# A hybrid decoder trunk on one core: where the sums of the down weights are made, when the last loads are issued, and which engine copies the exponentials

## The chip, the core and the metric

The kernel runs on one core of a Trainium2 chip. A core has five engines that work side by side: TensorE (PE in the profile; its weight loads are PEld), VectorE (DVE), ScalarE (ACT), GpSimd (POOL) and SyncE (SP), which in this kernel issues every DMA from one queue, in order. Each engine takes its instructions in the order in which the program put them. The metric is the device time of one execution in microseconds.

## The reference

One layer of a decoder trunk for 1024 tokens of width 1024, in float32. Three token mixers run on one projection of the normalised input: an attention with a forget bias ("FoX", 8 heads of 64), a diagonal state space ("S5") and a gated linear recurrence ("HGRN2"). Their outputs are merged with sigmoid gates, then come an output projection, a cross attention over 256 memory rows, and a SwiGLU of inner width 2816.

```python
def swiglu(h, w_gu, w_d):
    a, b = jnp.split(h @ w_gu, 2, axis=-1)
    return (jax.nn.silu(a) * b) @ w_d

merged = (gates[:, :, 0] * (y_fox @ wb[:BRANCH_W])
          + gates[:, :, 1] * (y_s5 @ wb[BRANCH_W:2 * BRANCH_W])
          + gates[:, :, 2] * (y_hg @ wb[2 * BRANCH_W:]))
x = x + merged @ w_out[l]
x = x + cross_attention(rmsnorm(x, norm_x[l]), rmsnorm(mem, norm_mem[l]), ...)
x = x + swiglu(rmsnorm(x, norm_ffn[l]), w_gate_up[l], w_down[l])
```

## The kernel before

**Numbers.** Every large product is made from two parts of each factor: ScalarE copies a tile to its rounded high part (`act(hi, src, AF.Copy)`, line 264), and VectorE subtracts it from the tile, which leaves the low part (line 267, through line 253 and 244). Three 128x512 matmuls (high by high, high by low, low by high) make one step (line 388, and line 1983 in the feed-forward stages). All additions and subtractions stand on line 244 in the profile, all ScalarE operations on line 241, all matmuls on line 226, so the rows are told apart by tile names.

**Order.** The program is one long list that a compiler pass turns into a fixed order for each engine. Main work is written as generators, and filler generators (projections) are stepped between their pieces by `drive` and `pump`, by a running sum of planned matmul time (`self.pe`, in which a 512-column matmul counts 0.215 us). `later(us, fn)` puts a piece of work in when that sum has grown by so many us. All tiles in SBUF that are named `u` share 50 buffers of 4 KB per partition. A load waits until a buffer is free, and SP stands still meanwhile.

**Attention stage** (`fox_main`, line 737; 320 to 630 us). Per head and half of the tokens, for each of 4 or 8 key blocks j: TensorE makes scores `st`, ScalarE takes their exponential into `pf` (line 778), GpSimd copies it to the high part `pt` (line 781), VectorE subtracts to the low part (line 784), GpSimd adds the exponential to a running sum `facc`, and two blocks later TensorE multiplies `pt` with the values (`pv`). Before a unit, maxima of the scores go through a short VectorE chain (`mc`), are transposed (`mt`) and copied by ScalarE into a row operand (`q12`). After a pair of units, `facc` is split into `ah` and summed over partitions by small matmuls (`sm`, line 834), which `later(2.0, sums)` puts in (line 841).

**Gated merge** (`gates`, `gate`, `glu`, lines 1608 to 1672; some 950 to 1100 us). For three branches and eight output blocks, a stored gate is loaded, multiplied with a branch projection and added to the merge tile `mg`. GpSimd adds the second branch, VectorE the third. The output projection (`residual`) and the cross attention follow.

**Feed-forward, up** (`ffn_up`, line 2109). Two gate/up blocks are computed directly. The other 20 go through a seven-product scheme on quadrants (`PRODUCTS`, line 28): weights a11, s1, s2, s4, s3, a12, a22 with activations b11, t1, t2, b22, t3, b21, t4. `ffn_mix` makes t1 to t4 and their parts (tiles `t`, `th`, `tl`), `unit_prep` the weight sums of one block (tiles `sa`, `sb`) and their parts `wc`. While a block runs (`up_unit`), `after(n)` follows its product n: it prepares the next block's weights, or, behind the last block, loads and splits hidden rows (`h_load`, `h_split`, chunks by `H_AT`) and the first down weights (`dn_load`, `dn_prep`). The hidden rows and their mixes are stored to DRAM by `h_pair`, `h_pair2` and `h_store`.

**Feed-forward, down** (`ffn_down`, line 2232). The same seven products with four output blocks each, 28 weight blocks of 11 steps. For the sums s1, s2, s4 and s3, `dn_load` loads two sources and `dn_prep` adds or subtracts them on GpSimd (tiles `wr`) before the split into `wc`. The sums s1 and s2 are stored to DRAM, as s2 and s4 are made from them:

```python
DN_SRC = {"s1": ("a21", "a22"), "s2": ("s1", "a11"), "s4": ("a12", "s2"), "s3": ("a11", "a21")}
```

## Time and profile before

| what | value |
|---|---|
| time, median of 3 runs | 2147.52 us (2146.33 to 2148.11) |
| the profiled execution | 2145.49 us |
| its span on the core | 2143.7 us |
| TensorE busy | 2073.8 us, 97% of the span |
| VectorE, ScalarE, GpSimd busy | 1525.9, 814.1, 610.7 us |
| DMA traffic | 245.18 MB, mean 114 GB/s |

The busy time of TensorE is made from modelled ends of pipelined matmuls, so short gaps don't show in it; the number of matmuls that start in a stretch shows them. An idle time is put down to the instruction whose end released the engine. Where a wait row names an engine, that is the last of the things waited for.

### The profile page before, as it was taken

To read this page: it belongs to the slowest core of one execution; us is meant where nothing else is said; L and a number is where in the kernel's file an instruction comes from. 1 tells how busy PE (TensorE), PEld (TensorE's weight loads), DVE (VectorE), ACT (ScalarE), POOL (GpSimd) and SP (SyncE) were. 2 spreads that over 40 slices of the span, in tenths; PEclk is the share of its full clock that TensorE was granted. 3 is DMA by queue.
4 is the path that set the end of the run, shared out by engine and by line. 5 is a ranking of instruction groups with operands and counts; after the bars stand their busy time and mean duration, and the time that the engine had idled before them with its cause. 6 is when DMAs were issued, how large, how long until landed. Compare 5 with 4: busy or idle time off the path is not lost.

```text
span 2143.7 us, 26772 instructions
## 1 busy us (share of the span) xinstructions
PE 2073.8 (97%) x10044; PEld 1701.3 (79%) x10044; DVE 1525.9 (71%) x2221; ACT 814.1 (38%) x1268; POOL 610.7 (28%) x495
## 2 busy tenths in 40 slices
PE   8998999999999999999999999999999999989899
PEld 5887776776788888887888888878788888878677
DVE  8888898889845576536665576756878787866764
ACT  4113355556421222216334455534433333334231
POOL 4281204455531111000603000011432232425740
PEclk9999999999999999999999999999999999999999
DMA  4332120110210121124434533243222232269783
GB/s 162 137 103 75 51 86 21 40 50 30 79 54 30 50 69 55 59 98 171 159 102 144 197 90 108 79 165 125 92 97 102 99 123 98 99 228 356 267 292 132
DMA packets 102610, 245.18 MB, mean 114 GB/s; under 512 B 15816, under 2 KB 32200, under 8 KB 102480
## 3 DMA queue, kind: packets, MB, share of 16 engines
q1 hardware_dynamic: 102480, 243.46, 32.9%
q8 instruction: 79, 1.29, 0.2%
q14 instruction: 51, 0.42, 0.1%
HBM read 184.83 MB, written 57.41 MB: 113 GB/s over the span
## 4 chain that ended last, share of the span: by engine, by line
PE 65%; DVE 4%; issue 1%; DMA 1%; ACT 1%; POOL 1%; SPq 0%; DVEq 0%; POOLq 0%; ACTq 0%
PE pj L226 32%; PE fp L226 26%; PE hs L226 2%; PE xo L226 1%; DVE wc L244 1%; PE rs L226 1%; PE xs L226 1%; DVE hl L244 1%; PE ho L226 1%; POOL t L244 0%; PE hst L226 0%; PE pv L226 0%; PE st L226 0%; DVE tl L244 0%; DMA hr<-hb_d 0%
## 5 line engine op out<-in xcount | busy, mean ns | idle before, releaser
L226 PE MATMUL pj<-xh,wh 128*128 128x512 f32 x784 | 312.8, 404 | 6.7 <-ACT xh L241 5.3
L226 PE MATMUL pj<-xl,wh 128*128 128x512 f32 x784 | 314.1, 404 | 3.5 <-DVE xl L256 3.4
L226 PE MATMUL pj<-xh,wl 128*128 128x512 f32 x784 | 310.4, 399 | 0.0
L226 PE MATMUL fp<-hh,wc 128*128 128x512 f32 x644 | 196.5, 397 | 15.9 <-DVE wc L244 13.2
L226 PE MATMUL fp<-th,wc 128*128 128x512 f32 x640 | 208.2, 391 | 2.2 <-ACT th L241 2.2
L244 DVE TENSOR_TENSOR wl<-wr,wh 128x1024 fp32r<-128x1024 f32 (+2 forms) x138 | 166.1, 1204 | 52.1 <-ACT wh L241 50.2
L226 PEld LDWEIGHTS pj<-xh,wh 128*128 128x128 f32 x784 | 148.9, 190 | 39.6 <-ACT xh L241 5.8
L226 PEld LDWEIGHTS pj<-xl,wh 128*128 128x128 f32 x784 | 148.0, 189 | 35.4 <-DVE xl L256 5.8
L226 PE MATMUL fp<-fx,wc 128*128 128x512 f32 x720 | 173.0, 389 | 0.0
L226 PEld LDWEIGHTS pj<-xh,wl 128*128 128x128 f32 x784 | 148.4, 189 | 30.7 <-issue 2.2
L241 ACT ACTIVATE wh<-wr 128x1024 fp32r<-128x1024 f32 (+2 forms) x138 | 131.6, 957 | 76.6 <-DMA wr<-w_in 39.6
L226 PEld LDWEIGHTS fp<-hh,wc 128*128 128x128 f32 x644 | 123.1, 192 | 44.7 <-DVE wc L244 15.8
L226 PEld LDWEIGHTS fp<-fx,wc 128*128 128x128 f32 x720 | 135.2, 188 | 28.1
L244 DVE TENSOR_TENSOR wc<-wr,wc 128x512 fp32r<-128x512 f32 (+1 forms) x116 | 119.7, 1054 | 40.9 <-ACT wc L241 40.9
L226 PEld LDWEIGHTS fp<-th,wc 128*128 128x128 f32 x640 | 120.9, 189 | 27.8 <-ACT th L241 2.7
L244 POOL TENSOR_TENSOR acc<-acc,sq 128x512 f32<-128x512 f32 (+1 forms) x18 | 30.8, 1709 | 375.5 <-ACT sq L241 375.4
L226 PE MATMUL fp<-tl,wc 128*128 128x512 f32 x320 | 125.3, 392 | 1.6 <-DVE tl L244 1.6
L244 DVE TENSOR_TENSOR pt<-pf,pt 128x512 fp32r<-128x512 f32 (+1 forms) x96 | 94.1, 983 | 39.6 <-POOL pt L260 39.3
L244 POOL TENSOR_TENSOR fc<-fc,fs 128x512 f32<-128x512 f32 x40 | 57.3, 1433 | 220.3 <-ACT fs L241 220.3
L226 PE MATMUL fp<-hl,wc 128*128 128x512 f32 x280 | 111.1, 397 | 0.0
L260 POOL TENSOR_SCALAR pt<-pf 128x512 fp32r<-128x512 f32 (+1 forms) x96 | 68.8, 717 | 136.4 <-ACT pf L241 126.0
L241 ACT ACTIVATE wc<-wr 128x512 fp32r<-128x512 f32 (+1 forms) x116 | 76.9, 699 | 64.4 <-POOL wr L244 47.4
(429 smaller groups left out, 4841.2 us busy)
## 6 DMA issues: line engine op xcount, KB each, us to landing
wr<-w_in SPq DMA_DIRECT2D x48, 512.0 KB, 4.1
wr<-w_gu SPq DMA_DIRECT2D x44, 512.0 KB, 4.1
wr<-w_dn SPq DMA_DIRECT2D x36, 512.0 KB, 7.1
hr<-hb_d SPq DMA_DIRECT2D x35, 512.0 KB, 6.7
hb_d<-fc SPq DMA_DIRECT2D x44, 256.0 KB, 2.1
gz_d<-gz SPq DMA_DIRECT2D x20, 512.0 KB, 2.9
gate<-gz_d SPq DMA_DIRECT2D x20, 512.0 KB, 3.7
wr<-xo SPq DMA_DIRECT2D x17, 512.0 KB, 4.9
```

Of the source, the lines that this page charges most:

```text
L226: self.nc.tensor.matmul(out, lhsT, rhs, start=start, stop=stop)
L241: self.nc.scalar.activation(out=out, in_=in_, func=f, **kw)
L244: return (eng or self.nc.vector).tensor_tensor(out=out, in0=a, in1=b, op=op)
L260: (eng or self.nc.vector).tensor_scalar(out=out, in0=a, scalar1=s1, scalar2=s2, op0=op0, **kw)
```

## The change

1. **Sums of the down weights.** A new function `dn_mix(n)` takes one output block and two row pairs: one load of all four quadrants, four GpSimd operations that make s1, s3, s2 and s4 in place, and 4 us of planned time later one store to the DRAM tensor `ws_d`. 24 of them run in a chain, 9 us of planned matmul time apart, from the point behind the last `hg_main` on, while the first branch is being merged. `dn_load` then loads one source for every block, from `ws_d` or from the input, and `dn_prep` only splits. The stores of s1 and s2 and `dkeep` are gone.
2. **End of the up stage.** The loads of down block 0 and of the first two hidden chunks are issued before the last gate/up block, those of the other chunks one product earlier than before; the loads of blocks 1 and 2 come behind products 1 and 3; blocks 0 and 1 are split behind products 2 and 4. The b11 rows of a pair are stored at the end of the even block.
3. **Start of the up stage.** The four weight sums of the first scheme block are made on GpSimd, and the mixes 2 and 3 both follow the second block of the second half.
4. **Attention stage.** All high parts of exponentials are copied by ScalarE instead of GpSimd, and the row sums `sm` come 6 us instead of 2 us of planned time behind their unit.

```diff
-H_AT = {0: (0, 1), 1: (2,), 2: (3,), 3: (4,), 4: (5,)}
+H_AT = {-1: (0, 1), 0: (2,), 1: (3,), 2: (4,), 3: (5,)}
-DN_SRC = {"s1": ("a21", "a22"), "s2": ("s1", "a11"), "s4": ("a12", "s2"), "s3": ("a11", "a21")}
+MIXED = {"s2": 0, "s4": 1, "s3": 2, "s1": 3}
+SUM_AT = 6.0
+MIX_AT = (4.0, 9.0)
...
-                if j % 4 in self.hi_pool:
-                    self.ts(pt[:, 0, q0:512], pr, 1.0, 0.0, ALU.mult, ALU.add, self.nc.gpsimd)
-                else:
-                    self.act(pt[:, 0, q0:512], pr, AF.Copy)
+                self.act(pt[:, 0, q0:512], pr, AF.Copy)
...
-            self.later(2.0, sums)
+            self.later(SUM_AT, sums)
...
+        self.ws_d = self.dp.tile([4, 4, P, NPR, P], F32, name="ws_d")
+        self.later(MIX_AT[1], lambda: self.dn_mix(0))
         zt = []
...
-    def unit_prep(self, j):
+    def unit_prep(self, j, eng=None):
...
-        self.add(sa[:, 0], a21, a22)
+        self.add(sa[:, 0], a21, a22, eng)
...
                 else:
                     self.heven = c1
+                    self.h_store("b11", j // 2, c11)
...
-        prep = self.unit_prep(FF_CONV)
+        prep = self.unit_prep(FF_CONV, self.nc.gpsimd)
...
-                elif i < 3:
-                    self.ffn_mix(i + 1)
-                    next(prep)
+                elif i < 2:
+                    for m in ((1,), (2, 3))[i]:
+                        self.ffn_mix(m)
+                        next(prep)
...
+                if n in (1, 3):
+                    self.dn_load((n + 1) // 2)
                 for c in H_AT.get(n - 1, ()):
                     self.h_split("b11", c)
-                if n in (0, 2, 4):
-                    self.dn_load(n // 2)
-                if n == 4:
-                    self.dn_prep(0)
-
+                if n in (2, 4):
+                    self.dn_prep(n // 2 - 1)
+
+            if prep is None:
+                self.dn_load(0)
+                for c in H_AT[-1]:
+                    self.h_load("b11", c)
             yield from self.up_unit(j, after)
...
+    def dn_mix(self, n):
+
+        ob, k = n // 6, 2 * (n % 6)
+        m = min(2, NPR - k)
+        t = self.u("dm", F32, (P, 4, 2, P))
+        self.nc.sync.dma_start(out=t[:, :, 0:m], in_=self.io["w_dn"][ob][:, :, k:k + m].rearrange("q p k m -> p q k m"))
+        a11, a12, a21, a22 = (t[:, q, 0:m] for q in range(4))
+        G = self.nc.gpsimd
+        self.add(a22, a21, a22, G)
+        self.sub(a21, a11, a21, G)
+        self.sub(a11, a22, a11, G)
+        self.sub(a12, a12, a11, G)
+
+        def store():
+            self.nc.sync.dma_start(out=self.ws_d[ob][:, :, k:k + m].rearrange("q p k m -> p q k m"), in_=t[:, :, 0:m])
+        self.later(MIX_AT[0], store)
+        if n + 1 < 24:
+            self.later(MIX_AT[1], lambda: self.dn_mix(n + 1))
...
-        if a in DN_SRC:
-            op = ALU.add if a == "s1" else ALU.subtract
-            self.tt(big[0], big[0], big[1], op, self.nc.gpsimd)
-            self.tt(rem[:, 0], rem[:, 0], rem[:, 1], op, self.nc.gpsimd)
-            if a in self.ws_d:
-                self.dkeep.append((a, ob, big[0], rem))
```

## Rows read from the trace of the kernel before

**Rows 1.** The page's first part: busy us, share, instructions of each engine.
```profile
PE 2073.8 (97%) x10044; PEld 1701.3 (79%) x10044; DVE 1525.9 (71%) x2221; ACT 814.1 (38%) x1268; POOL 610.7 (28%) x495
```

**Rows 2.** Table of stretches: PE, PEld, DVE, ACT, POOL busy (started), clock, DMA share, GB/s.
```profile
500.00:550.00 50.00, 46.00 (x216) 36.09 (x216) 45.41 (x65) 25.09 (x43) 28.54 (x32) 1.00 0.09 32
950.00:1000.00 50.00, 49.73 (x226) 40.10 (x225) 26.50 (x39) 28.87 (x39) 0.00 (x0) 1.00 0.46 165
1000.00:1050.00 50.00, 50.00 (x222) 41.39 (x221) 35.79 (x39) 23.94 (x33) 32.89 (x14) 1.00 0.57 195
1500.00:1550.00 50.00, 46.19 (x196) 37.48 (x195) 44.47 (x53) 20.41 (x29) 22.65 (x13) 0.97 0.21 74
1600.00:1650.00 50.00, 50.00 (x222) 41.44 (x221) 40.08 (x53) 16.28 (x28) 19.14 (x13) 1.00 0.34 122
```

**Rows 3.** Tile fp, matmuls: min/median/max ns, first and last start us, shapes.
```profile
L226 PE MATMUL fp<-fx,wc x720: 387/389/397, 1519.8 to 1903.7; 128*128 128x512 f32 x180
L226 PE MATMUL fp<-hh,wc x644: 387/389/792, 1909.5 to 2139.4; 128*128 128x512 f32 x161
L226 PE MATMUL fp<-th,wc x640: 388/389/628, 1522.5 to 1906.4; 128*128 128x512 f32 x160
```

**Rows 4.** TensorE's waits, 1900 to 2144 us: total us, times, longest.
```profile
PE fp L226 <- DVE wc L244: 13.2, 6, 3.8
PE fp L226 <- ACT wc L241: 2.7, 1, 2.7
```

**Rows 5.** Table of stretches, columns as in rows 2: the hand-over.
```profile
1910.00:1920.00 10.00, 6.23 (x18) 4.76 (x18) 6.60 (x7) 1.99 (x3) 2.18 (x1) 0.66 0.97 324
```

**Rows 6.** Groups by form, 1906 to 2060 us: busy, mean ns, idle before, releasers.
```profile
L244 DVE TENSOR_TENSOR hl<-hr,hh 128x1024 fp32r<-128x1024 f32 x22 | 36.6, 1688 | 0.0
L244 DVE TENSOR_TENSOR wc<-wr,wc 128x1024 fp32r<-128x1024 f32 x19 | 35.6, 1872 | 25.4 <-ACT wc L241 25.4
...
L244 POOL TENSOR_TENSOR wr<-wr 128x1024 f32<-128x1024 f32 x15 | 39.8, 2656 | 57.3 <-DMA wr<-w_dn 52.9 <-DVE hl L244 4.4
```

**Rows 7.** Timeline at 1519 to 1531 us: start, length, instruction, idle before.
```profile
1526.97 0.50 PE L226 MATMUL fp<-th,wc 128*128 128x512 f32 x1 [2.25 <-ACT th L241]
...
1527.02 4.19 DVE L244 TENSOR_TENSOR tl<-t,th 128x1024 fp32r<-128x1024 f32 x2
...
1519.41 2.21 POOL L244 TENSOR_TENSOR t<-xr,t 128x512 f32<-128x512 f32 x1 [4.24 <-DVE t L244]
```

**Rows 8.** Groups by form in the attention stage, 320 to 630 us, three engines.
```profile
L244 DVE TENSOR_TENSOR pt<-pf,pt 128x512 fp32r<-128x512 f32 x48 | 62.0, 1294 | 31.1 <-POOL pt L260 30.9
...
L244 DVE TENSOR_TENSOR ah<-facc,ah 128x512 fp32r<-128x512 f32 x16 | 11.8, 740 | 0.2
...
L260 POOL TENSOR_SCALAR pt<-pf 128x512 fp32r<-128x512 f32 x48 | 36.5, 763 | 63.2 <-ACT pf L241 58.2 <-DVE ah L244 2.2 <-DVE pt L244 1.5
...
L244 POOL TENSOR_TENSOR facc<-facc,pf 128x256 f32<-128x256 f32 x16 | 11.8, 736 | 1.4 <-ACT pf L241 1.4
...
L241 ACT ACTIVATE ah<-facc 128x512 fp32r<-128x512 f32 x16 | 10.0, 625 | 0.7 <-DVE pt L244 0.5
```

**Rows 9.** TensorE's waits in the attention stage, 320 to 630 us.
```profile
PE sm L226 <- DVE ah L244: 8.1, 5, 2.3
PE mt L231 <- DVE mc L244: 7.9, 9, 1.7
...
PE pv L226 <- POOL pt L260: 0.5, 1, 0.5
```

**Rows 10.** The merge, 945 to 1200 us: a wait of SP's queue; a GpSimd group.
```profile
SPq L1601 <- DVE hoT L244: 25.8, 1, 25.8
...
L244 POOL TENSOR_TENSOR mg<-mg,gate 128x512 f32<-128x512 f32 x16 | 38.8, 2453 | 156.0 <-DVE gate L244 155.8 <-ACT yh L241 0.2
```

**Rows 11.** DMA issues: count, KB each, median us from issue to landing.
```profile
wr<-w_dn SPq DMA_DIRECT2D x36, 512.0 KB, 7.1
...
gate<-gz_d SPq DMA_DIRECT2D x20, 512.0 KB, 3.7
```

More of the change, by code (lines that the diff above doesn't have):

```diff
@@ L733, in fox_pre @@
         return out + [chain, rows]
-    hi_pool = (0, 1, 2, 3)
     def fox_main(self):
@@ L1430, in run @@
         self.hb_d = self.dp.tile([7, NPR, P, 512], F32, name="hb_d")
-        self.ws_d = {n: self.dp.tile([4, P, NPR, P], F32, name=f"{n}_d") for n in ("s1", "s2")}
         self.filler("xo", self.out_proj())
@@ L2023, in unit_prep @@
         sa = self.u("sa", F32, (P, 2, 4, P))
-        self.add(sa[:, 0], a21, a22)
+        self.add(sa[:, 0], a21, a22, eng)
         parts("s1", sa[:, 0])
         yield
-        self.sub(sa[:, 1], sa[:, 0], a11)
+        self.sub(sa[:, 1], sa[:, 0], a11, eng)
         parts("s2", sa[:, 1])
@@ L2030, in unit_prep @@
         sb = self.u("sb", F32, (P, 2, 4, P))
-        self.sub(sb[:, 0], a12, sa[:, 1])
+        self.sub(sb[:, 0], a12, sa[:, 1], eng)
         parts("s4", sb[:, 0])
         yield
-        self.sub(sb[:, 1], a11, a21)
+        self.sub(sb[:, 1], a11, a21, eng)
         parts("s3", sb[:, 1])
@@ L2093, in h_pair @@
         b11, b12, b22 = e[:, 0:512], e[:, 512:1024], o[:, 512:1024]
-        self.h_store("b11", i, b11)
         self.sub(ta[:, 0], b12, b11, G)
@@ L2150, in first @@
             ta, tb = self.u("ta", F32, (P, 2, 512)), self.u("tb")[:, 0:512]
+            self.h_store("b11", 0, e[:, 0:512])
             self.h_pair(0, e, o, ta)
@@ L2159, in ffn_up @@
         self.hraw, self.hx = {}, {b: [] for b in HX}
-        self.draw, self.dw, self.dkeep = {}, {}, deque()
+        self.draw, self.dw = {}, {}
         for j in range(FF_CONV, NFF):
@@ L2201, in dn_load @@
         a, ob = PRODUCTS[s // 4][0], s % 4
-        big, rem = [], self.u("wr", F32, (P, 2, 3, P))
-        for n, src in enumerate(DN_SRC.get(a, (a,))):
-            ap = self.ws_d[src][ob] if src in self.ws_d else self.io["w_dn"][ob][QUAD[src]]
-            big.append(self.u("wr", F32, (P, 8, P)))
-            self.nc.sync.dma_start(out=big[n], in_=ap[:, 0:8])
-            self.nc.sync.dma_start(out=rem[:, n], in_=ap[:, 8:NPR])
+        big, rem = self.u("wr", F32, (P, 8, P)), self.u("wr", F32, (P, 3, P))
+        ap = self.ws_d[ob][MIXED[a]] if a in MIXED else self.io["w_dn"][ob][QUAD[a]]
+        self.nc.sync.dma_start(out=big, in_=ap[:, 0:8])
+        self.nc.sync.dma_start(out=rem, in_=ap[:, 8:NPR])
         self.draw[s] = big, rem
     def dn_prep(self, s):
-        while self.dkeep:
-            a, ob, big, rem = self.dkeep.popleft()
-            self.nc.sync.dma_start(out=self.ws_d[a][ob][:, 0:8], in_=big)
-            self.nc.sync.dma_start(out=self.ws_d[a][ob][:, 8:NPR], in_=rem[:, 0])
-        if s >= 4 * len(PRODUCTS):
+        if s >= 4 * len(PRODUCTS) or s in self.dw:
             return
-        a, ob = PRODUCTS[s // 4][0], s % 4
         big, rem = self.draw.pop(s)
-        if a in DN_SRC:
-            op = ALU.add if a == "s1" else ALU.subtract
-            self.tt(big[0], big[0], big[1], op, self.nc.gpsimd)
-            self.tt(rem[:, 0], rem[:, 0], rem[:, 1], op, self.nc.gpsimd)
-            if a in self.ws_d:
-                self.dkeep.append((a, ob, big[0], rem))
         hi, lo = (self.u("wc", F32R, (P, 8, P)) for _ in range(2))
         r = self.u("wc", F32R, (P, 2, 3, P))
-        self.split(big[0], hi, lo)
-        self.split(rem[:, 0], r[:, 0], r[:, 1])
+        self.split(big, hi, lo)
+        self.split(rem, r[:, 0], r[:, 1])
         self.dw[s] = hi, lo, r
```

## The prediction

> **What bounds the kernel now.** I read the page first: TensorE is busy 2073.8 of 2143.7 us [rows 1], so only its idle time can be won, about 70 us. A busy share hides part of that, since a 128x512 matmul is recorded as 389 ns long [rows 3], so I counted starts. The table of stretches shows 222 starts in 50 us where nothing stops TensorE [rows 2], which is 0.2252 us each. Then I looked where the count falls or the engine idles: the attention stage (320 to 630 us), the first products of the gate/up blocks (1500 to 1550) and the down projection (1900 to the end). The gated merge (950 to 1100) runs at 50.00 of 50 from 1000 on: TensorE is its bound, and VectorE, ScalarE and GpSimd have room there [rows 2]. Last I read who ended TensorE's idle time in each place, and what that engine did.
>
> The two feed-forward stages can be counted exactly. The up products are 20 blocks of 84 matmuls, 1680, from 1519.8 to 1906.4 and the length of one pitch [rows 3]: 1680 x 0.2252 = 378.3 us of 386.8, so 8.5 us are lost. The down products are 28 blocks of 33, 924 matmuls, which follow until 2139.4 [rows 3]: 924 x 0.2252 = 208.1 of 233.0, so 24.9 us are lost. Of these the wait rows name 13.2 + 2.7 [rows 4]. The rest is smaller gaps, and the clock: between 1910 and 1920, after idling, the granted clock was 0.66 and 18 matmuls started [rows 5], where 44 is the full rate. A stop costs more than its own length here.
>
> **Down projection: sums made earlier, second loads and stores gone.** Today 16 of the 28 weight blocks (s1, s2, s4, s3) are added from two loads on GpSimd before they are split. These sums took 2.66 us for 128x1024, and waited mostly for weight loads; VectorE's low part, which waits for ScalarE's high part, which waits for the sum, took 1.87 us [rows 6]. These low parts are what TensorE waits for [rows 4]. The change removes 32 GpSimd instructions, 16 second loads and 8 stores of 704 KB, about 17 MB, from a stage whose DMA share was 0.97 in the stretch shown [rows 5]. What remains per block of 33 x 0.2252 = 7.43 us is one 704 KB load, a ScalarE split and two VectorE low parts, 1.87 us and, for the 128x384 remainder, no more than that. VectorE's other work is six subtractions for hidden rows per product of four blocks, 1.5 per block at 1.69 us or less [rows 6]. Together that is 6.3 us of 7.43 at today's stretched durations, so nothing is late next in steady state.
>
> **Down projection: its beginning.** Of the 24.9 us the hand-over at 1906 to 1918 is the largest piece. The load of weight block 0 and of the first two hidden chunks moves ahead of the last gate/up block, whose 84 x 0.2252 = 18.9 us then cover it. The loads of blocks 1 and 2 and of the other hidden chunks move one product (2.7 us) earlier. The split of block 0 moves from the fifth product to the third, and block 1 is split inside this stage as well. On SP's queue these loads pass the stores of the last pair, which now stand ahead of some of them. The stores of b11 move to the end of the even block, where SP can stand until product 7 is evacuated; what is queued behind is the next weight load, three products away, so it costs nothing. VectorE gets two more low parts in these 18.9 us, but no next block is prepared then. I keep 3.4 us lost of 24.9 and take **-21.5 us**. Bounds: -24.9 (no loss left), and -11 if only the steady part or only the beginning is cured.
>
> **First up products.** TensorE stops for 2.25 us on the mixed activations th, then on tl, and VectorE's last two subtractions of that mix end only at 1531.2, sharing time with GpSimd [rows 7]. The change takes four VectorE additions for the first block away and puts them on GpSimd, at up to 2.21 us each by its row of that form [rows 7]. It issues mixes 1, 2 and 3 after the first and second matmul block instead of the first, second and third, 24 x 0.2252 = 5.4 us earlier for the last. Needed are 4.2 us (1531.2 less 1527.0, when TensorE wanted the first of them), and GpSimd is busy 22.65 of 50 us there [rows 2]. I take **-5 us** of 8.5; bounds +2 (GpSimd's additions queue ahead of its part of the mixes) and -8.5.
>
> **Attention stage: ScalarE copies.** GpSimd's 96 copies (a 512 one took 0.763 us) go to ScalarE, where the same form of copy took 0.625 us [rows 8]. Half of them are 512 wide, 48 x 0.625 = 30 us; the others are 128 to 384 wide, between 0 and 30 us, say 20. ScalarE is busy 25.1 of 50 us [rows 2]; 50 us more over 310 us make it about 33. VectorE's subtraction behind it took 1.294 us, while the same form in another place took 0.740 [rows 8]; at most 48 x 0.55 = 27 us of VectorE time come free, and GpSimd's running sum of the same tiles stays, so I count on half. TensorE itself waited only 0.5 us for these copies [rows 9]: it gains through VectorE's order. It waited 7.9 us for mc, a short chain on VectorE [rows 9]; I take half, 4 us. On ScalarE the next exponential and the row copies q12 queue behind each new copy, 0.6 us. The row sums sm, which cost 8.1 us because VectorE had not yet written ah, with 2.3 us the longest [rows 9], are issued 4 us of matmul time later (SUM_AT 2 to 6); I take all 8 us. Together **-12 us**. Bounds: +2 if every unit's rows come later (16 units x 0.6 = 10 us given back, and nothing for mc), and -25 if VectorE's relief also closes gaps too short for the wait rows.
>
> **Gated merge: the cost.** 24 mixes are added, each one load and one store of 512 KB at most (11.5 MB each way) and four GpSimd instructions of 128x256: 0.736 us each by the nearest form [rows 8], 1.23 by half of the strided 512 add that took 2.45 us in this stage [rows 10]; 71 to 118 us in all, over some 250 us. Each takes one of 50 buffers for a while, and SP issues it between the gate and weight loads. TensorE is what hides it, and SP has stood still 25.8 us on one store here [rows 10], in a stretch in which TensorE was still busy 49.73 of 50 [rows 2]. I take **+2.5 us**; bounds 0 and +25.
>
> Where GpSimd works beside it, VectorE's subtraction of two SBUF tiles is stretched from 0.740 to 1.294 us [rows 8]. The Trainium skill (SBUF — State Buffer, section "Who interferes with whom") says that a VectorE instruction with two SBUF inputs and a GpSimd instruction that reads SBUF exclude each other. The trace agrees in direction; by that rule the new sums delay VectorE in the merge, which is rival (d).
>
> **Sum.** -21.5 - 5 - 12 + 2.5 = -36.0 us. The profiled execution took 2145.49 us (span 2143.7, the rest around it) and gives 2109.5; the median of the runs is 2.0 above it, so **2111.5 us**.
>
> **Rivals.** (a) ScalarE takes GpSimd's place in the attention stage: rows and exponentials are late behind the copies, and the stage comes out at its +2: 2125.5. For it: ScalarE is in order and its work rises by a third. Against: it has 17 of 50 us left. (b) VectorE is freed more than I count, -25 there: 2098.5. For it: 1.294 against 0.740. (c) The down stage is cured by half, since hidden rows or the first blocks are late instead of sums: +10.5, 2122. (d) VectorE becomes the merge's bound: it is busy 26.5 and 35.8 us per 50 [rows 2], some 156 of 250; if 118 us of GpSimd time shut it out in full, that is 274, 24 more than there is, 2133 to 2135. Against: the lower price gives 227, which fits. (e) Slower: SP's queue becomes the pace of the merge. SP waits in order, so between a mix's load and its store it may issue nothing: a landing of 3.7 us as for the gates or 7.1 as in the crowded down stage [rows 11], 2.9 to 4.9 us of sums, and up to one add of 2.45 ahead of them, 6.6 to 14.5 us. Mixes come every 9 us of planned matmul time, in which a 512 matmul counts 0.215: with 0.2252 and half a step of 1.4 us that is 10.1. At 13.5 us the queue falls behind by 3.4 x 24 = 82 us; less a lead of 25.8 us that is 56 us: 2165. It makes the kernel slower than before from 12.8 us per mix. Against it: loads are issued far ahead here, as the 25.8 us show.
>
> **Chances.** Forecast 0.52, (a) 0.15, (b) 0.13, (c) 0.07, (d) 0.06, (e) 0.07. Range: 2096 to 2131, which takes in (a), (b), (c) and most of the forecast's bounds, and leaves out (d) and (e), 0.13, with some of the tails. A measurement of this kernel tells about 0.2%, 4 us. Faster 0.91, same 0.03 (an (e) that just balances), slower 0.06.
>
> **What will show it.** The starts from the first to the last down product should span about 211 us, with a DMA share well below 0.97 and no granted clock near 0.66. The two stops on th and tl should shrink under 2 us together. In the attention stage sm should leave TensorE's waits, VectorE's 512 subtraction should fall to about 1.0 us, and ScalarE should be busy about 33 of 50. In the merge the busy time per 50 us should stay as it is. I am wrong if q12 or pf take over in the attention stage, if weight loads end TensorE's idle time in the merge, or if wc still ends it in the down stage.

## The result and the profile after

The changed kernel takes **2232.03 us** (median of 4 runs, 2230.73 to 2234.11) against 2147.82 before (4 runs): a ratio of 1.0384, interval 1.0363 to 1.0405. It is slower by 84 us where 36 us of gain were forecast. Its profiled execution took 2232.75 us, with a span of 2230.9.

The page of after, busy time and two of its 40 slices:

```profile
PE 2077.9 (93%) x10044; PEld 1705.4 (76%) x10044; DVE 1493.2 (67%) x2217; ACT 860.2 (39%) x1364; POOL 566.6 (25%) x467
...
PE   8998999899999999990299999999999999999999
...
PEclk9999999999999999995599999999999999999999
```

TensorE does the same 10044 matmuls in nearly the same busy time as in [rows 1], and its share falls from 97% to 93%: the new time is idle time, and the slices say where. Two of them, the 19th and 20th from the left, have almost no matmul in them, at half the granted clock. That is the gated merge. The table of stretches there (columns as in [rows 2]; the x of a stretch counts every instruction that lies in it, also those that began before it or end behind it), and who ended the waits of TensorE and of ScalarE:

```profile
990.00:1050.00 60.00, 15.77 (x66) 11.72 (x64) 11.35 (x14) 6.66 (x9) 31.43 (x47) 0.67 0.67 214
1050.00:1100.00 50.00, 0.00 (x0) 0.00 (x0) 0.00 (x0) 0.00 (x0) 30.41 (x46) 0.50 0.65 203
...
PE pj L228 <- ACT wh L243: 96.0, 1, 96.0
...
ACT wh L243 <- DMA wr<-w_glu: 88.7, 1, 88.7
```

In [rows 2] the same place has 222 matmuls in 50 us. Here one stop of 96.0 us stands: TensorE waits for ScalarE's high part of a weight block, and ScalarE waits 88.7 us for that block's load. For fifty microseconds only GpSimd works. The load isn't slow; it has not been issued. SP's queue in order of time (start, length, instruction), and its waits from 990 to 1110:

```profile
992.13 0.38 SPq L348 DMA_DIRECT2D wr<-w_glu  x1
...
993.39 2.82 SPq L2207 DMA_DIRECT2D dm<-w_dn  x3
1003.83 6.61 SPq L2216 DMA_DIRECT2D ws_d<-dm  x3
...
1097.84 1.85 SPq L2216 DMA_DIRECT2D ws_d<-dm  x2
1099.74 1.03 SPq L348 DMA_DIRECT2D wr<-w_glu  x2
...
SPq L2216 <- POOL dm L246: 59.8, 23, 3.7
...
SPq L2216 <- DMA dm<-w_dn: 18.5, 7, 3.9
```

Between one weight load at 992.13 and the next at 1099.74 SP issues nothing but the loads and stores of the mixes, and stands at the stores for 59.8 + 18.5 us. But for the load of the first one, at 964.53, all 24 mixes lie in one block of the queue, ahead of the weights that TensorE needs next.

The reason can be read in the code. The mixes are started with `later`, each of them puts the next one on the same list, and the next `finish()` that is called without a tag flushes that list:

```python
    def tick(self, flush=False):
        while True:
            due = [x for x in self.late if flush or x[0] <= self.pe]
            if not due:
                return
```

With `flush` the due time isn't looked at, and the loop goes on until the list is empty. The first `self.finish()` behind the start of the merge therefore runs mix 0, its store, mix 1, its store, and so on to mix 23 at a single point of the program. The description of the change, a chain in steps of 9 us of planned time, is what the constants say and not what the code does.

The rest of the profile, by stage. The table gives the start of a matmul in each trace less the start of the same matmul before, split into what each stage adds (us): the attention up to the last scores matmul, the stage behind it up to the last ho, the merge up to the last yh product, from there to the first matmul xs of the cross attention, the cross attention up to the first up product, the up products, the down products. "Ahead" is what had gathered at the first scores matmul. Up to there the kernels that differ only behind it run the same program, and yet lie between 0.0 and +2.9, so that 2 to 3 us of a single trace are not read as an effect; what returns in several kernels is.

| kernel | ahead | attention | to ho | merge | to xs | to up | up | down | sum |
|---|---|---|---|---|---|---|---|---|---|
| after | +1.7 | 0.0 | +5.2 | **+100.6** | +1.1 | 0.0 | +2.3 | **-23.5** | +87.3 |
| e1_spread | +1.4 | -1.0 | +5.2 | +22.7 | +22.0 | +1.6 | +1.1 | -23.5 | +29.5 |
| e7_late_store | +0.5 | -2.1 | +6.7 | +22.6 | +5.5 | +1.6 | +1.0 | -23.5 | +12.2 |
| e10_three_steps | +0.5 | -1.0 | +5.2 | +19.9 | +6.6 | 0.0 | +2.3 | -23.5 | +10.0 |
| e8_pool_store | +2.1 | -0.9 | +6.7 | +19.1 | +1.5 | 0.0 | +2.2 | -23.5 | +7.2 |
| e14_no_sums | +2.0 | -1.0 | +6.8 | **+2.0** | +3.9 | 0.0 | +1.1 | -23.5 | -8.8 |
| e11_best | +2.9 | -4.4 | +4.8 | +20.8 | +5.5 | +1.6 | +0.7 | -23.5 | +8.4 |
| e12_mix_in_cross | +1.7 | -4.5 | +4.9 | 0.0 | +0.1 | +5.7 | -0.3 | -23.5 | **-15.9** |
| e16_down_only | +2.8 | +1.6 | 0.0 | 0.0 | 0.0 | +8.4 | -0.2 | -23.5 | -10.9 |
| e2_act_only | +0.6 | -4.5 | +3.2 | 0.0 | +0.2 | +1.5 | 0.0 | +1.6 | +2.7 |
| e3_sum_only | +2.9 | +4.5 | +5.1 | 0.0 | 0.0 | 0.0 | -0.1 | +1.4 | +13.8 |
| e5_up_start | +0.4 | 0.0 | 0.0 | 0.0 | 0.0 | 0.0 | +1.1 | +1.4 | +2.8 |
| e15_mix_order | 0.0 | 0.0 | +0.1 | 0.0 | +0.5 | 0.0 | -0.7 | +0.2 | -0.1 |

**Down.** This part did what was meant. The tiles of the up and down products in after (as in [rows 3]), three stretches of the down stage, and under them the 50 us of the hand-over in the kernel before:

```profile
L228 PE MATMUL fp<-hh,wc x644: 388/389/389, 2017.4 to 2226.7; 128*128 128x512 f32 x161
...
L228 PE MATMUL fp<-th,wc x640: 388/389/628, 1631.0 to 2017.2; 128*128 128x512 f32 x160
...
2000.00:2050.00 50.00, 50.00 (x222) 41.44 (x221) 33.36 (x33) 24.26 (x33) 10.51 (x7) 1.00 0.80 287
2030.00:2040.00 10.00, 10.00 (x46) 8.29 (x45) 4.64 (x5) 3.86 (x5) 0.00 (x0) 1.00 1.02 378
2040.00:2050.00 10.00, 10.00 (x46) 8.29 (x45) 4.28 (x5) 5.86 (x9) 0.00 (x0) 1.00 1.04 391
```

```profile
1900.00:1950.00 50.00, 43.54 (x181) 35.19 (x181) 33.58 (x28) 19.79 (x28) 25.19 (x14) 0.93 0.91 332
```

The hand-over has no gap (2017.2, then 2017.4), the full count of 222 in 50 us stands from the first stretch, and the longest matmul of that group took 389 ns where [rows 3] had 792. From the last up product to the last down product there are 209.5 us instead of 233.0: 23.5 us won, in this and in every kernel of the table that has the part. That is all there was to win: 924 matmuls in 209.5 us are one per 0.2267 us, and the trace has three starts per 0.68 us where nothing stops TensorE. The DMA share was not what held the stage: over 50 us it is 0.80 where the kernel before has 0.91, but two stretches of 10 us reach 1.02 and 1.04 with no matmul lost. How much of the 23.5 us is the sums made earlier and how much the loads issued earlier was not run apart.

**Attention and up products.** Neither gained. TensorE's waits from 320 to 630 in after, VectorE's subtraction there, two stretches of it, the longest stop of the stage behind, and the first waits of the up products (1620 to 1660):

```profile
PE mt L233 <- DVE mc L246: 4.4, 6, 1.3
PE mx L228 <- DVE pmx L709: 3.3, 1, 3.3
PE pv L228 <- DVE pt L246: 2.7, 3, 2.1
...
PE sm L228 <- DVE ah L246: 1.6, 1, 1.6
...
L246 DVE TENSOR_TENSOR pt<-pf,pt 128x512 fp32r<-128x512 f32 x48 | 48.9, 1022 | 25.7 <-ACT pt L243 25.4
...
410.00:420.00 10.00, 7.92 (x29) 5.68 (x30) 7.59 (x18) 3.67 (x7) 1.36 (x3) 0.66 0.13 52
...
440.00:450.00 10.00, 6.75 (x27) 5.43 (x26) 9.30 (x14) 2.25 (x4) 3.35 (x3) 0.83 0.01 2
...
PE hst L228 <- ACT hbT L243: 3.0, 1, 3.0
...
PE fp L228 <- ACT th L243: 3.4, 1, 3.4
PE fp L228 <- DVE tl L246: 1.6, 1, 1.6
```

The signs that were named came: sm fell from 8.1 to 1.6 us and the 512 subtraction from 1.294 to 1.022 us [rows 8, 9]. The time didn't: mx and pv wait instead, two stretches ran at a granted clock of 0.66 and 0.83 where the kernel before has 1.00, and a stop of 3.0 us on hbT is new.

### The profile page after: what moved, and what is told of

It is laid out like the page before. It is cut to its first block, busy times and chain, and to the rows that moved or that the text cites. A ratio compares the mean times of both kernels' runs of the same rounds, so it can differ in the third digit from the quotient of the medians.

```text
span 2230.9 us, 26945 instructions
## 1 busy us (share of the span) xinstructions
PE 2077.9 (93%) x10044; PEld 1705.4 (76%) x10044; DVE 1493.2 (67%) x2217; ACT 860.2 (39%) x1364; POOL 566.6 (25%) x467
## 3 DMA queue, kind: packets, MB, share of 16 engines
q8 instruction: 79, 1.29, 0.2%
## 4 chain that ended last, share of the span: by engine, by line
PE 55%; POOL 3%; DVE 3%; DMA 2%; ACT 1%; issue 0%; SPq 0%; POOLq 0%; ACTq 0%; DVEq 0%
PE fp L228 26%; PE pj L228 24%; POOL dm L246 3%; DMA dm<-w_dn 2%; PE hs L228 1%; PE xo L228 1%; PE xs L228 1%; PE rs L228 1%; PE ho L228 0%; DVE tl L246 0%; DVE xr L258 0%; DMA wr<-xv 0%; DVE fx L246 0%; PE xt L233 0%; PE hst L228 0%
## 5 line engine op out<-in xcount | busy, mean ns | idle before, releaser
L243 ACT ACTIVATE wh<-wr 128x1024 fp32r<-128x1024 f32 (+2 forms) x138 | 131.7, 957 | 165.2 <-DMA wr<-w_glu 88.7
L228 PE MATMUL fp<-hh,wc 128*128 128x512 f32 x644 | 191.5, 389 | 0.0
L246 DVE TENSOR_TENSOR wc<-wr,wc 128x512 fp32r<-128x512 f32 (+1 forms) x116 | 107.1, 942 | 31.3 <-ACT wc L243 31.3
L246 POOL TENSOR_TENSOR dm<-dm 128x256 f32<-128x256 f32 (+1 forms) x96 | 64.8, 685 | 165.9 <-DVE wl L246 106.0
L228 PE MATMUL pj<-zh,wh 128*128 128x512 f32 x32 | 13.5, 425 | 96.0 <-ACT wh L243 96.0
L246 POOL TENSOR_TENSOR facc<-facc,pf 128x256 f32<-128x256 f32 (+1 forms) x64 | 71.1, 1110 | 119.8 <-ACT pf L243 114.0
```

What stands on the lines that cost most here:

```text
L228: self.nc.tensor.matmul(out, lhsT, rhs, start=start, stop=stop)
L243: self.nc.scalar.activation(out=out, in_=in_, func=f, **kw)
L246: return (eng or self.nc.vector).tensor_tensor(out=out, in0=a, in1=b, op=op)
```

## The experiments

Two questions were open. Is the slowdown the order (the flush, SP's queue), or the work (GpSimd's sums, the transfers)? And do the parts without the mixes give what was forecast? The theory after the comparison was: the flush makes nearly all of it, and without it the change is worth some 30 us. The rival: the work itself doesn't fit into the merge.

### The flush taken away

e1_spread: the mixes get a list of their own, which goes by the due time alone.

```diff
+    def spread(self, us, fn):
+        self.slow.append((self.pe + us, fn))
...
             due = [x for x in self.late if flush or x[0] <= self.pe]
+            due += [x for x in self.slow if x[0] <= self.pe]
...
-        self.later(MIX_AT[0], store)
+        self.spread(MIX_AT[0], store)
```

> The changed kernel, with the 24 mixes on a list of their own that is due by planned matmul time alone and that the end of the first branch does not flush; all else as in the change. Theory 1 (the flush put all mixes in one block ahead of the next weight loads on SP's queue): TensorE's 96 us wait in the merge goes, the time is 2232 less about 102, so 2128 to 2136. Theory 2 (the mixes themselves cost, through GpSimd time, shared SBUF access or DMA traffic in the merge): spread out they cost the same sum, and the time stays above 2180.

Measured: 2175.14 us (4 runs), ratio 1.0117, interval 1.0099 to 1.0136, between the two theories. So the flush alone is worth some 57 us of the 84, and the kernel is still slower than before. SP's waits of 990 to 1340 in e1_spread:

```profile
SPq L2222 <- POOL dm L246: 93.9, 22, 8.7
SPq L2222 <- DMA dm<-w_dn: 89.8, 21, 9.2
```

SP stands 183.7 us at 24 stores, 7.7 us each, with the weight and gate loads behind it. The stores came from 991.3 to 1263.8, one per 11.8 us, where the plan wanted one per 10.1. This is the wait of rival (e) of the prediction, SP at a store in front of loads; what it costs is shown by the kernels that take it away.

### SP kept from standing still

Three kernels take the waiting away from SP in three ways. e7_late_store issues the store 15 us of planned time behind the load; e10_three_steps moves the sums behind the load as well; e8_pool_store issues the store on GpSimd's own queue.

```diff
-MIX_AT = (4.0, 9.0)
+MIX_AT = (15.0, 9.0)          # e7_late_store
...
-        self.spread(MIX_AT[0], store)
+        self.spread(12.0, sums)   # e10_three_steps, with MIX_AT = (24.0, 9.0)
+        self.spread(MIX_AT[0], store)
...
-            self.nc.sync.dma_start(out=self.ws_d[ob][:, :, k:k + m]...
+            G.dma_start(out=self.ws_d[ob][:, :, k:k + m]...   # e8_pool_store
```

> The changed kernel with the mixes spread over the merge as in e1_spread, and each mix's store put on SP's queue 15 us of planned time behind its load instead of 4, so that the sums are done when SP comes to it. Nothing else differs: the same bytes, the same GpSimd work. Theory A (what is left of the slowdown in e1_spread, 2175.1 us, is SP standing in front of a store whose sums GpSimd has not made yet, with weight and gate loads queued behind it): SP's waits for GpSimd's dm, 93.9 us in the stretch 990 to 1340 of e1_spread, fall under 20 us, and the shift against the kernel before at the start of the first up product falls from +52 to about +10; 2130 to 2140 us. Theory B (the price is the work itself: 24 loads and stores of 0.5 MB and 96 operations on GpSimd beside VectorE in a stage that has no room): the shift stays at +40 to +55, 2165 to 2180 us.

> As e7_late_store, but also the four sums are put on GpSimd's queue only 12 us of planned time behind the load, and the store 24 us behind it: neither GpSimd nor SP then waits for a transfer of the mixes. Theory A: the waits of GpSimd for dm's load, 116.3 us in 990 to 1340 of e1_spread, fall under 30 us too, and the gated merge's own operations on GpSimd are no longer behind them; 5 to 10 us faster than e7_late_store, 2122 to 2135 us. Theory B: no difference from e7_late_store.

> The mixes spread as in e1_spread, with the store issued from GpSimd's own queue right behind the sums, so that SP never sees it. Theory A: as e7_late_store within 5 us, 2125 to 2145 us. Theory B (contention for GpSimd, the shared memory or the transfers): 2165 to 2180 us as e1_spread.

Measured: 2157.97 us (1.0038, 1.0024 to 1.0053), 2157.56 us (1.0039, 1.0028 to 1.005) and 2151.25 us (1.0004, 0.9991 to 1.0017), the kernel before at 2148.78 beside them. e7 and e8 lie between their two theories; e10 came out on its theory B, no difference from e7. By the table the stretch behind the merge got its 22.0 us back (to 5.5, 6.6 and 1.5), and the merge itself kept 19 to 23 us in all three. So SP's standing at the stores, from which e8 is free, cost some 20 us behind the merge and 3 to 4 us in it. In e7 and e10 SP's waits for GpSimd didn't fall as expected: they are 92.4 and 90.0 us where e1 has 93.9. In e10 (a stretch, one of SP's waits of 990 to 1340, SP's queue, and TensorE's longest wait):

```profile
1040.00:1090.00 50.00, 38.89 (x156) 30.48 (x154) 27.79 (x27) 12.92 (x15) 35.98 (x28) 0.86 0.55 188
...
SPq L2224 <- POOL dm L246: 90.0, 21, 9.6
...
1053.70 7.42 SPq L2224 DMA_DIRECT2D ws_d<-dm  x2
1061.21 1.94 SPq L1682 DMA_DIRECT2D ldy<-hy_d  x3
...
PE pj L228 <- ACT yh L243: 7.8, 1, 7.8
```

The sums come late however late the store is put, since GpSimd has its own part of the merge to do in the same queue. SP reaches two stores at 1053.70, gets past them at 1061, and only then issues three loads of branch outputs; TensorE stopped at 1059 for 7.8 us (8.2 us in e7), waiting for yh, which is made from them.

In e8 SP never sees a store of the mixes, and TensorE stops all the same: one stop of 10.2 us in place of 7.8. The stretch, TensorE's wait and SP's two waits in e8, then VectorE's low part of the branch outputs (1020 to 1130 in e8, under it 1020 to 1110 in the kernel before):

```profile
1040.00:1090.00 50.00, 38.48 (x160) 30.71 (x160) 43.92 (x27) 7.30 (x8) 47.47 (x37) 0.90 0.56 199
...
PE pj L228 <- ACT wh L243: 10.2, 1, 10.2
...
SPq L1682 <- POOL mg L246: 19.1, 2, 11.9
...
SPq L353 <- POOL mg L246: 11.3, 1, 11.3
...
L246 DVE TENSOR_TENSOR yl<-ldy,yh 128x1024 fp32r<-128x1024 f32 x4 | 10.4, 2595 | 0.0
```

```profile
L244 DVE TENSOR_TENSOR yl<-ldy,yh 128x1024 fp32r<-128x1024 f32 x4 | 5.0, 1257 | 0.0
```

GpSimd is busy 47.47 of 50 us. Loads now wait until GpSimd has done its merge additions mg, and VectorE, which reads two SBUF tiles beside it, is stretched from 1.257 to 2.595 us. So GpSimd is the common part of all three: in e7 and e10 through stores whose sums are late, in e8 through loads whose buffers its merge additions still hold, and through VectorE.

### The sums left out

> e10_three_steps with the four sums of each mix left out: the loads and the stores of the mixes stay on SP, 24 us of planned time apart, and the down weights are stored as they came. GpSimd does nothing for the mixes. Theory A (what still costs 20 us in the merge of e10_three_steps is GpSimd's time: its own queue, VectorE stretched beside it, and SP waiting for it): the last matmul of the merge that reads yh comes within 5 us of e10's start of the merge plus the 109 us of the kernel before, a shift of +5 to +9 against the kernel before, where e10_three_steps has +24.6; about 2136 us. Theory B (the transfers, 24 MB more in a stage that moved 116 to 202 GB/s): the shift stays above +18, about 2150 us.

```diff
         def sums():
-            self.add(a22, a21, a22, G)
-            self.sub(a21, a11, a21, G)
-            self.sub(a11, a22, a11, G)
-            self.sub(a12, a12, a11, G)
+            pass
```

Measured: 2136.59 us (one run), as theory A has it. The merge's loss falls from +19.9 (e10_three_steps) to +2.0, with the same transfers in it. The same stretches in e14:

```profile
990.00:1040.00 50.00, 48.54 (x214) 39.83 (x213) 34.81 (x44) 30.37 (x43) 15.01 (x7) 1.00 0.91 319
1040.00:1090.00 50.00, 49.51 (x217) 40.33 (x216) 35.73 (x41) 15.52 (x19) 22.55 (x10) 1.00 0.80 265
```

A DMA share of 0.91 costs little here (214 matmuls in the first stretch, 222 being the full count), and 217 matmuls lie in the second stretch where e10 had 156. The shift up to the end of the merge is +9.7, 0.7 us over what theory A allowed, and +7.7 of it was there before the merge began. So GpSimd's time is some 18 us of the 19.9 that the merge lost in e10; the transfers, and the buffers that the mixes hold, are at most 2.0 us of it. (How much of the 18 is GpSimd's own queue and how much VectorE stretched beside it was not separated.) The Trainium skill (SBUF — State Buffer, "Who interferes with whom") says that transfers use ports of their own and don't hold up compute engines; this stretch agrees. The same section's rule, VectorE with two SBUF inputs excluded by GpSimd's reads, was the base of rival (d), and the 2.595 us above agree with it in direction.

### The other parts by themselves

e2_act_only is the kernel before with ScalarE's copies, e3_sum_only with SUM_AT at 6.0, e5_up_start with the whole start of the up products, e15_mix_order with its earlier order alone.

```diff
-                if j % 4 in self.hi_pool:
-                    self.ts(pt[:, 0, q0:512], pr, 1.0, 0.0, ALU.mult, ALU.add, self.nc.gpsimd)
-                else:
-                    self.act(pt[:, 0, q0:512], pr, AF.Copy)
+                self.act(pt[:, 0, q0:512], pr, AF.Copy)        # e2_act_only
...
-            self.later(2.0, sums)
+            self.later(6.0, sums)                              # e3_sum_only
...
-                elif i < 3:
-                    self.ffn_mix(i + 1)
-                    next(prep)
+                elif i < 2:                                    # e5_up_start, e15_mix_order
+                    for m in ((1,), (2, 3))[i]:
+                        self.ffn_mix(m)
+                        next(prep)
...
-        prep = self.unit_prep(FF_CONV)
+        prep = self.unit_prep(FF_CONV, self.nc.gpsimd)         # e5_up_start alone
```

> The kernel before, with the high parts of the exponentials copied by ScalarE and nothing else. Theory 1 (ScalarE's order gives back what VectorE gains): 2146 to 2156, with TensorE's waits moving from mc to pv and mx. Theory 2 (the forecast's: VectorE is freed, a gain of 4 us): 2140 to 2145. In the changed kernel the whole stretch up to the merge was 6.9 us longer; if the copies are the cause, 2153 to 2156.

> The kernel before, with the row sums 6 us instead of 2 us of planned matmul time behind their unit and nothing else. Theory 1 (the forecast's: their wait for ah goes and nothing takes its place): 2138 to 2141. Theory 2 (the wait moves to other work of the same chains): 2146 to 2149.

> The kernel before, with the first scheme block's weight sums on GpSimd and the mixes 2 and 3 both behind the second block, nothing else. Theory 1 (the forecast's): the stops on th and tl go, 2142 to 2144. Theory 2 (as in the changed kernel, where the up stage was only 0.6 us shorter: GpSimd's part of the mixes now ends last): 2146 to 2149.

> The kernel before with one half of the change at the start of the up products: ffn_mix 1 to 3 in two steps instead of three, as in the change, with the additions of the weights' sums staying on VectorE. Theory A (in e5_up_start the gain of the earlier order is eaten by those additions, which stand on GpSimd's queue ahead of its share of the mixes): the stops at the start of the up products, 2.63 and 2.07 us before, shrink by 1.5 us or more in sum. Theory B (the order alone gives nothing, since VectorE's own mixes are what ends last): 2.5 and 2.0 us as before. The time is within 5 us of the kernel before either way.

Measured: e2 2146.09 us (0.9983, 0.9972 to 0.9994), e3 2159.22 us (1.0038, 1.0018 to 1.0058), e5 2150.76 us (1.0002, 0.9987 to 1.0018), all against 2150.48 beside them; e15 2145.39 us (one run). So the copies give 0.2%, some 4 us: theory 2 by the ratio, though beside this kernel before the time itself lies at the lower end of theory 1's range. The later sums cost 0.4%, which neither theory allowed, and the start of the up products gives nothing, as theory 2 has it.

The copies win 4.4 to 4.5 us in the attention in all three kernels that have them without the later sums (e2, e11, e12), and lose 3.2 to 4.9 us in the stage behind. No wait there explains that; the granted clock does, which fell between 760 and 790 in all three: what it lacked to 1.00 over these three stretches of 10 us comes to 3.4 us in e2, 5.1 in e11 and 5.2 in e12, where 3.2, 4.8 and 4.9 were lost. Two of the stretches in e2:

```profile
760.00:770.00 10.00, 10.00 (x54) 8.15 (x53) 5.08 (x8) 0.14 (x1) 0.97 (x1) 1.00 0.16 66
770.00:780.00 10.00, 10.00 (x34) 7.68 (x34) 5.01 (x8) 1.55 (x2) 1.56 (x1) 0.66 0.01 2
```

TensorE is busy in all of it, and yet the clock falls to 0.66 in the second stretch. Why it falls there and not in the kernel before is open.

The 4.5 us themselves came by another wait than the prediction named: in e2 the waits for sm fell from 8.1 to 2.7 us and those for mc only from 7.9 to 6.9.

The later sums take sm out of the waits, and put others in. TensorE's waits from 320 to 630 in e3:

```profile
PE pv L226 <- DVE pt L244: 4.0, 6, 1.4
PE mx L226 <- DVE pmx L707: 3.2, 1, 3.2
...
PE sm L226 <- DVE ah L244: 0.9, 1, 0.9
```

TensorE's waits from 320 to 630 come to 19.4 us in all, against 19.2 before: they moved and didn't shrink. VectorE works its queue in order and is the late one there; a later due time for one consumer only lets another one meet it. The 4.5 us that e3 lost in the attention are no longer waits but again the clock: 0.76, 0.90, 0.96 and 0.87 in four stretches of 10 us between 410 and 460, 5.1 us in sum, where the kernel before has 1.00. In the stage behind, the stop of 3.0 us on hbT is there in e3 as in after.

At the start of the up products, GpSimd's share of the mixes comes later in e5, behind the additions that were given to it and behind VectorE. GpSimd's queue and VectorE's in e5 (start, length), and under them VectorE's in the kernel before; [rows 7] has the last of GpSimd's lines at 1519.41:

```profile
1516.23 2.27 POOL L244 TENSOR_TENSOR sb<-wr 128x512 f32<-128x512 f32 x1
...
1521.49 2.21 POOL L244 TENSOR_TENSOR t<-xr,t 128x512 f32<-128x512 f32 x1 [1.29 <-DVE t L244]
...
1517.28 1.77 DVE L244 TENSOR_TENSOR t<-xr 128x512 f32<-128x512 f32 x1
1518.98 1.77 DVE L244 TENSOR_TENSOR wc<-sb,wc 128x512 fp32r<-128x512 f32 x1
1520.67 0.68 DVE L244 TENSOR_TENSOR t<-xr,t 128x512 f32<-128x512 f32 x1
```

```profile
1517.38 0.68 DVE L244 TENSOR_TENSOR t<-xr 128x512 f32<-128x512 f32 x1
...
1518.59 0.68 DVE L244 TENSOR_TENSOR t<-xr,t 128x512 f32<-128x512 f32 x1
```

GpSimd stood idle for 1.29 us before its line at 1521.49, until VectorE's t at 1520.67 was done. VectorE is late there, 2.08 us behind the kernel before (0.4 of it from the start of the trace), though it has two additions less to do: the same subtraction that took 0.68 us while GpSimd was idle takes 1.77 beside GpSimd's additions, and so does the next one.

The stop on th grew from 2.25 to 3.37 us there. In e15, without those additions on GpSimd, it is 1.66 us and the stop on tl 1.50 (1.56 before), 0.65 us less in sum and the up stage 0.7 us shorter: neither theory, and no more than a single trace can tell, but nearer to "the order gives nothing", as VectorE's last two low parts still take 4.20 us where [rows 7] has 4.19.

### A better place for the mixes

e11_best is e10_three_steps without the later sums and the new start of the up products. e12_mix_in_cross leaves the merge alone and starts the mixes with the cross attention, where GpSimd has next to nothing to do, with the stores on GpSimd's queue. e16_down_only is e12 without ScalarE's copies: the down part alone.

```diff
-        self.spread(MIX_AT[1], lambda: self.dn_mix(0))        # at the start of the merge
...
         self.finish("xq0")
+        self.spread(MIX_AT[1], lambda: self.dn_mix(0))        # e12, e16: MIX_AT = (4.0, 8.0)
         self.pump(X_PRE)
```

> e10_three_steps without the other two parts that gave nothing or cost something by themselves: the sums of the attention at 2.0 us as before (at 6.0 they cost 8 us in e3_sum_only), and the start of the up products as before (e5_up_start gave nothing). ScalarE's copies and the down part stay. Theory A, from the parts: 2147.8 of the kernel before, less 23.5 in the down stage, less 4 of the copies, plus up to 10 for the mixes: 2120 to 2132 us, faster than both kernels. Theory B: 2150 to 2165 us.

> The down part and ScalarE's copies of the change, with the sums of the attention and the start of the up products as before, and the 24 mixes put elsewhere: from the start of the cross attention on, 8 us of planned time apart, the store issued from GpSimd's own queue. In the kernel before GpSimd is idle from 1180 to 1380 and busy 5.6 to 7.4 of 40 us from 1380 to 1500, at a DMA share of 0.29 to 0.56. Theory A (the slowdown was a matter of the place and the order: in the merge GpSimd has work of its own that TensorE waits for, and SP's queue has loads that come just in time): the mixes cost 0 to 4 us here, the down stage gives 23.5 and the copies 0 to 4; 2120 to 2130 us, faster than both kernels. Theory B (96 operations on GpSimd and 24 MB of transfers cost some 20 us wherever they stand): 2140 to 2150 us.

> The down part of the change alone, with the 24 mixes in the cross attention and their stores on GpSimd's queue as in e12_mix_in_cross; the attention is that of the kernel before, GpSimd's high parts among it. Theory A (the copies on ScalarE give nothing that lasts: in e2_act_only they gained 3.9 us up to the last scores matmul, of which 0.7 were left at the end of the next stage): as e12_mix_in_cross within 3 us, 2126 to 2132 us. Theory B (the copies' 4 us stand): 2132 to 2135 us. Either way the run prices the down part by itself: 23.5 less the 5.8 us that the cross attention lost in e12_mix_in_cross, of which part came back behind it.

Measured: e11 2151.58 us (1.0004, 0.999 to 1.0018), on theory B, as the merge kept its 20.8 us. **e12 2129.83 us** (6 runs), ratio **0.9921**, interval 0.9908 to 0.9934, and e16 2133.06 us, ratio 0.9917, interval 0.9902 to 0.9933, each against the kernel before measured beside it (2147.66 and 2149.85). Both are faster than both kernels, than the one before by 17 to 18 us, 0.8%. e12 is on its theory A; e16 has the time of theory B and the ratio of theory A. GpSimd's sums cost as much time as ever; groups of 1180 to 1520, and TensorE's longest wait there, in e12:

```profile
L246 POOL TENSOR_TENSOR dm<-dm 128x256 f32<-128x256 f32 x80 | 74.4, 930 | 120.1 <-DMA dm<-w_dn 102.5 <-DVE acc L258 6.8 <-PE xs L228 5.9
L2220 POOL DMA_DIRECT2D ws_d<-dm x24 | 18.7, 777 | 7.1 <-POOL dm L246 6.8 <-DMA dm<-w_dn 0.3
...
PE xs L228 <- ACT xp L243: 2.3, 1, 2.3
```

With the 16 narrower sums (9.3 us) that is 102 us of GpSimd time, and the stage loses 5.7 us (8.4 in e16), where nearly the same work cost 20 in the merge. Since the ratios of e12 and e16 agree within their intervals, the copies give nothing there that can be measured; a gain of e2's size, 0.2%, is at the edge of what the two intervals could show.

## Why the prediction was wrong

Term by term, as the prediction put them (profiled execution, us):

| term | predicted | bounds | in after | alone or elsewhere |
|---|---|---|---|---|
| down | -21.5 | -24.9 to -11 | -23.5 | -23.5 in every kernel with it |
| first up products | -5 | -8.5 to +2 | +2.3 | e5 +1.1, e15 -0.7 |
| attention | -12 | -25 to +2 | +5.2 (+1.7 ahead of it) | e2 -1.3, e3 +9.6, to the last ho |
| merge | +2.5 | 0 to +25 | +101.7 | +2.0 without the sums (e14) |

+1.7 + 5.2 + 101.7 + 2.3 - 23.5 = 87.4, and the profiled executions lie 2232.75 - 2145.49 = 87.3 apart.

**The step that failed** is the merge term's "over some 250 us", the overlap that was to make the mixes cost +2.5 us and at most +25; it cost 101.7. The spacing behind it is one sentence of rival (e): "Mixes come every 9 us of planned matmul time". I read the distance off the constants and didn't follow what `finish` does with the list that holds it. By the code the distance is zero: the whole chain is issued where the first flush stands. Rival (e) named the right queue and the right wait, SP in order at a store whose sums are not there yet. It was worked out as a queue that falls behind by some microseconds per mix, priced at 2165 and given a chance of 0.07. What stood against it, a lead of 25.8 us in SP's queue [rows 10], was no lead any more: the weight load behind the block was issued 107 us after the one ahead of it.

**The price of the merge** would have been wrong without the flush too. Its "TensorE is what hides it" counted room on GpSimd, 32.89 busy of 50 [rows 2], as if room were a price of zero. With the mixes spread the merge lost 19 to 23 us (e1, e7, e8, e10), of which e14 shows 18 to be the sums. Rival (d) named GpSimd's sums as the cause, and the 24 us that it adds are about the size of the loss, but its path, VectorE as the merge's bound, is only part of it: in the stretch from 1040 VectorE was busy 43.92 of 50 us in e8 and only 27.79 in e10, where SP waited for GpSimd's queue. The duration was as the bounds had it: 0.73 us for a 128x256 sum with little else running (after), 0.93 to 1.09 in company (e12, e10, e8), where 0.736 to 1.23 were given.

**The attention** failed at "I take all 8 us" of sm: the wait went, but VectorE, which was late, is in order, and mx, pv and hbT met it later, and the clock fell; with SUM_AT alone the kernel is slower by 0.4%. The prediction argued from whom TensorE waits for, and a wait that falls on another consumer of the same late engine is not a gain. The copies did what was said of them on VectorE (1.022 us) and won 4.5 us where 4 were taken, but by sm more than by mc, so that two terms counted on one wait; and most of it was lost again at the granted clock in the next stage, for which the prediction had no term. Rival (a), ScalarE too slow, wasn't it: ScalarE was busy 206.31 us of 310, about the 33 of 50 forecast, and TensorE's waits for its q12 were 1.8 and 0.9 us in all.

**The up products** went to the upper bound that was written beside the term, "GpSimd's additions queue ahead of its part of the mixes", and that names half of the way: the wait that ends last is for VectorE, stretched from 0.68 to 1.77 us beside these additions. The likelier end was chosen by GpSimd's busy share over 50 us, 22.65, where what counted was what the two engines did to each other in the 10 us before the stop. There was also less to win than the 8.5 us named: at 0.2267 us per matmul, 1680 of them take 380.9 of the 386.8 us, and 5.9 were lost.

**Down** was right in size, 209.5 us where about 211 were named, and no wait row is left. The pitch of 0.2252 us was a little short, since the 222 "starts" of [rows 2] include matmuls that began before the stretch (220 start in it); so 23.5 us were lost before and not 24.9, and none were kept. The sign "a DMA share well below 0.97" didn't come for stretches of that length (1.02 and 1.04), and TensorE didn't need it.

## What to carry to other kernels

Before a chain of small jobs is added to a planner, follow what each flush in the program does to it: a job that enters its own successor on the list comes out as one block, and on an in-order queue that block stands ahead of everything that is needed next. Room on an engine is not a place for work if that engine also has a part of the critical stage; price the new work where the engine is idle, and if a stage with an idle engine exists, put it there. When one engine is late for several consumers, moving one consumer moves the wait, so test such a step by itself. And work taken off VectorE for GpSimd can come back as longer VectorE instructions: look at their lengths where the two run side by side.

## What the runs showed of the hardware that was not expected

The granted clock fell to 0.66 in a stretch of 10 us in which TensorE was busy 10.00 of 10 and had not stopped in the 10 us before (e2, 770 to 780, 34 matmuls in it where the kernel before had 55), and to 0.76 in the same stretch of e12 and 0.84 in that of e11. In [rows 5] a low clock had stood behind idle time; here none is to be seen. The starts do show what TensorE did just before: from 769.29 to 772.50 in e2 matmuls that write 8 rows (fb) and 128 rows (pj) take turns and start some 0.4 us apart, where the others there start 0.23 us apart; then 16 small ones (hs) take 3.51 us, and 1.89 in the kernel before. But the kernel before has the same turns (773.13 to 776.34) at a clock of 1.00, so the cause is open.

While nothing else ran, in the 50 us without a matmul, the clock stood at 0.50, the lower of its two levels, and at 0.91 in the 50 us that followed.

A store issued from GpSimd's queue took 0.777 us of GpSimd's time (24 of them, e12), about as much as one of the sums. SP's queue shows 0.37 to 0.38 us for nearly every such store (e1).
